# One VectorE rotation for queries and keys, a stabiliser load in four parts, and a written order for the last mLSTM head

## The chip, the core and the metric

The kernel runs on one core of one Trainium2 chip. The metric is the device time of one execution in microseconds; of several executions of a kernel the median is taken. The core has five instruction streams that matter here: TensorE (PE: matmuls, PEld: their weight loads), VectorE (DVE), ScalarE (ACT), GpSimd (POOL) and SyncE (SP), which issues nearly all DMAs. Each engine works through its own stream in order, and waits on semaphores for the others.

## The reference, cut to what matters

One layer of a diffusion backbone: 1024 latent tokens and 256 context tokens of width 1024. After a modulated RMS norm, one projection feeds two groups of heads: a bidirectional chunkwise mLSTM (4 heads of 128) and a windowed attention (8 query heads and 2 key heads of 64). Then w_out, a gated residual, and a ConvGLU of width 2816. The change touches the mLSTM, and the rotary embedding of the attention:

```python
def apply_rope(x, cos, sin):
    b, l, h, _ = x.shape
    xr = x.astype(jnp.float32).reshape(b, l, h, 2, 2, ROPE_AXIS_PAIRS)
    x0, x1 = xr[..., 0, :], xr[..., 1, :]
    cs, sn = cos[:, None], sin[:, None]
    y = jnp.stack([x0 * cs - x1 * sn, x0 * sn + x1 * cs], axis=-2)
    return y.reshape(b, l, h, ATTN_DH).astype(x.dtype)
...
    m_t = jnp.maximum(a_log, jnp.max(d_log, axis=-1))
    dec = jnp.exp(d_log - m_t[..., None])
    inter = jnp.exp(a_log - m_t)
    s = jnp.einsum('bhntd,bhnsd->bhnts', q, k) * dec
...
        y_a = window_attention(apply_rope(qa, cos, sin) * attn_scale, apply_rope(ka, cos, sin), va,
                               ka_c, va_c, attn_sink[l])
```

## The kernel before

Tokens lie in ten chunks of 128: two of context, eight of latents (`NC` = 2, `NL` = 8, `NCH` = 10). A matrix product is made of three (`mm3`: high x high, high x low, low x high parts), so a weight slice arrives raw (`wr`), ScalarE casts the high part (`wh`, L153) and VectorE subtracts the low one (`wl`, L154), each half of a slice apart.

Stages, in us from the start of the span: up to 58 the norms and a first projection; 58 to 100 the second half of the projection of keys, values and gates (`px_mm`, `px_out`), beside the start of head 0's own projections; about 130, 195 and 265 the starts of mLSTM heads 0, 1 and 2, each beside the projections of the next head (`dense`); 334 head 3 (`mlstm(3)`) beside the first query projections (`qgen`); about 369 to 412 the rest of the query projections; from 412 attention and w_out, then the ConvGLU up to 1307.

*`px_out(c)`* evacuates a projected chunk from PSUM: gates on VectorE, `kv` on ScalarE. For latent chunks ScalarE copies the key into `kr`, GpSimd multiplies it with the cosine and sine tables (`rope`) into `ta`, and subtracts and adds the halves into `kv`, which is stored to `kv_d`. Before the projections' second half GpSimd also makes the modulated `ym` (L292) from which VectorE takes the low part `hl` (L297).

*`mlstm(h)`* is a generator of 30 steps: two transpositions ahead (`tr`, L644), nine backward state updates (index `i`; TensorE `pn` L671, VectorE `cst` or `cbk` L679/L681, which the next matmuls need), two forward steps over the context, one `first`, and two for each latent chunk. Its decay tiles `ee` are a broadcast of the stabilisers' rows `m_d`, loaded at its start (L641), masked (`mask`, L654) and exponentiated (`decay`, L658) block by block.

*Between the steps* the loop over heads takes pieces from the generator `dn`: `debt` grows by `rate` at each step (twice at the first), and a piece costs 0.64 if it is six matmuls of a query projection. For heads 0 to 2 `rate` is `RATE` = 1.5; for head 3 it is `RATE3`. In heads 0 to 2 most steps also advance `ada_second`, which loads 256 KB of `w_ada` and multiplies it into `acc` on VectorE (L812, L814).

*`qproj(i, b)`* projects query block `b` of half `i` (24 matmuls of 128x256 in four pieces) and rotates it; `qtrans` splits it into high and low parts `qs`, transposes it (`pt`, L870) and stores it to `q_d` (`QTo`). The 16 blocks come in the order of `qseq`: four of half 0, four of half 1, and so on, so the fifth is the first that needs `w_q[1]`. That slice is loaded at step `LW3` (12) by `late`; its source buffer takes the place of tiles freed at the head's start, and so does the rotated query tile `z`. `row_d` is a 16 KB store of the gate rows (`arw`) just before.

Up to head 2 TensorE, VectorE, ScalarE, GpSimd and SyncE run in the order in which the code is written; in head 3, and up to the last query projection, TensorE alone does, and a scheduler places the others.

Of the kernel before, what the change touches and what calls it, by code (L numbers as in the profile page):

```python
# [73 lines left out]
def build(tc, I, out, dbg=None):  # L74
# [243 lines left out]

    def px_out(c):
# [5 lines left out]
        else:  # L325
            S.copy(kv[:, P:], px[:, 16 + P:XW])
            kr = xp.tile([P, P], F32, name="kr", tag="kr")
            S.copy(kr[:], px[:, 16:16 + P])  # L328
            ta = xp.tile([P, 2, P], F32, name="ta", tag="ta", bufs=1)
            for i in range(2):  # L330
                G.tensor_tensor(out=ta[:, i].rearrange("p (h e) -> p h e", h=KVH),
                                in0=kr[:].rearrange("p (h e) -> p h e", h=KVH),
                                in1=rope[:, i, c - NC].unsqueeze(1).broadcast_to([P, KVH, ADH]), op=ALU.mult)
            tv = ta[:].rearrange("p i (a s j) -> p i a s j", s=2, j=16)
            kvv = kv[:, :P].rearrange("p (a s j) -> p a s j", s=2, j=16)
# [505 lines left out]
    def qproj(i, b):  # L841
# [10 lines left out]
        ta = xp.tile([P, 2 * P], F32, name="ta3", tag="ta", bufs=1)
        q4 = qt.rearrange("p (h e) -> p h e", h=4)
        rp_ = lambda j: rope[:, j, b].unsqueeze(1).broadcast_to([P, 4, ADH])
        G.tensor_tensor(out=ta[:].rearrange("p (h e) -> p h e", h=4), in0=q4, in1=rp_(1), op=ALU.mult)  # L855
        V.tensor_tensor(out=q4, in0=q4, in1=rp_(0), op=ALU.mult)
        tv = ta[:].rearrange("p (a s j) -> p a s j", s=2, j=16)
        qv = qt.rearrange("p (a s j) -> p a s j", s=2, j=16)
        G.tensor_tensor(out=qv[:, :, 0], in0=qv[:, :, 0], in1=tv[:, :, 1], op=ALU.subtract)
        G.tensor_tensor(out=qv[:, :, 1], in0=qv[:, :, 1], in1=tv[:, :, 0], op=ALU.add)  # L860
# [84 lines left out]
    for h in range(H):  # L945
        order_ = {mybir.EngineType.PE}
        if h + 1 < H:
            order_ |= {mybir.EngineType.DVE, mybir.EngineType.Activation, mybir.EngineType.Pool, mybir.EngineType.SP}
        else:
# [16 lines left out]
        with tc.manual_schedule(engines=order_):  # L966
            dn = dense(h + 1, wkq, wvo, *nh) if nh else qgen()
            rate = RATE if nh else RATE3
            for n, _ in enumerate(mlstm(h, *cur)):
# [21 lines left out]
            if nh is None:  # L991
                mstk.close()
                plk.close()
                pl = pT = pa_.enter_context(tc.tile_pool(name="pT", bufs=2, space=PSUM))
                pO = pa_.enter_context(tc.tile_pool(name="pO", bufs=1, space=PSUM))
                pU = pa_.enter_context(tc.tile_pool(name="pU", bufs=1, space=PSUM))
                wm = rstk.enter_context(tc.tile_pool(name="wm", bufs=1, side="right"))
                kT2 = [wm.tile([P, KVH, NCH * P], F32R, name=f"kT2{i}") for i in range(2)]
                vv = wm.tile([P, NCH, KVH, P], F32R, name="vv")
                S.activation(vv[:, 0, 0, 0:1], eps_t[:], AF.Exp)  # L1000
                kgens += [kprep(c) for c in range(NCH)]
                loads += [lambda: load_vv(0), lambda: load_vv(1), lambda: wos.append(load_wo(0, V, wm))]
            for _ in dn:
                pass
# [1042 lines left out]
```

## Time and profile before

| | |
|---|---|
| median of 3 runs | 1310.68 us (1309.24 to 1312.76) |
| the profiled execution | 1308.92 us |
| its span (first to last instruction) | 1306.9 us |
| mean granted TensorE clock | 0.992 |
| busy: PE, PEld, DVE, ACT, POOL | 96%, 82%, 75%, 49%, 19% |

The times of the trace are those of one execution and count from the first instruction of its span. A wait row reads "engine line <- what ended the wait"; PEclk is the granted clock of TensorE as a share of 2.4 GHz.

### The profile page before, as it was taken

The numbers are of one execution on the slowest core, as the hardware profiler recorded it, in microseconds if no ns is written. First come the engines' busy times: TensorE is split into PE (matmuls) and PEld (weight loads), VectorE is DVE, ScalarE is ACT, GpSimd is POOL, SyncE is SP. The second block draws the span as 40 slices with busy tenths as digits, with TensorE's granted clock in tenths as the row PEclk, the third lists the DMA queues.
The fourth block names the chain that finished last, engine by engine and source line by source line (L and its number), as shares of the span: only waits on it lengthen the run. The fifth ranks groups of instructions, "written<-read, shape, count | busy, mean of one in ns | idle before, by whom it ended". The sixth has DMA issues, their size and how long they took to land.

```text
span 1306.9 us, 19479 instructions
## 1 busy us (share of the span) xinstructions
PE 1255.5 (96%) x7071; PEld 1068.6 (82%) x7071; DVE 980.7 (75%) x1752; ACT 635.3 (49%) x1295; POOL 253.1 (19%) x252
## 2 busy tenths in 40 slices
PE   6999999999898999999989999999999999999997
PEld 4789998989898777878768788888888888788886
DVE  5754777777665888897898777777777776867887
ACT  6632546464764666776664333333333333434435
POOL 1240000000134223332411222222212222001000
PEclk9999999999998999999989999999999999999999
DMA  9431535362245322211422333322322326975653
GB/s 362 169 117 35 156 116 149 106 174 73 66 144 179 113 66 97 78 69 64 147 97 97 105 105 105 112 99 105 104 97 105 105 105 235 340 283 165 202 199 130
DMA packets 90226, 175.64 MB, mean 134 GB/s; under 512 B 12746, under 2 KB 29330, under 8 KB 90130
## 3 DMA queue, kind: packets, MB, share of 16 engines
q1 hardware_dynamic: 89842, 173.61, 39.7%
q8 instruction: 56, 0.92, 0.3%
q10 hardware_dynamic: 288, 0.79, 0.2%
q14 instruction: 40, 0.33, 0.1%
HBM read 136.04 MB, written 38.33 MB: 133 GB/s over the span
## 4 chain that ended last, share of the span: by engine, by line
PE 53%; DVE 8%; ACT 3%; DMA 2%; issue 2%; POOL 1%; SPq 0%; ACTq 0%; DVEq 0%; POOLq 0%
PE pd L1892 14%; PE pc L1384 8%; PE pa L1384 8%; PE pe L1384 4%; PE pb L1384 4%; PE pd L1384 4%; PE u L1154 2%; PE po L301 2%; PE po L303 2%; PE po L302 1%; DVE nm L1102 1%; PE pt L1131 1%; DMA ar<-act_s 1%; DVE nm L1103 1%; PE pf L1384 0%
## 5 line engine op out<-in xcount | busy, mean ns | idle before, releaser
L1486 ACT CAST wh<-Rb 128x1024 fp32r<-128x1024 f32 (+1 forms) x66 | 59.5, 904 | 144.6 <-PE pd L1384 81.6
L1892 PE MATMUL pd<-dh,al 128*128 128x512 f32 x296 | 115.5, 390 | 0.8 <-DVE al L1258 0.8
L1892 PE MATMUL pd<-dl,ah 128*128 128x512 f32 x296 | 115.4, 390 | 0.0
L1892 PE MATMUL pd<-dh,ah 128*128 128x512 f32 x296 | 115.3, 389 | 0.0
L1384 PE MATMUL pc<-hB,wh 128*128 128x512 f32 x344 | 106.5, 391 | 1.1 <-DVE av L1463 1.1
L1384 PE MATMUL pa<-hB,wh 128*128 128x512 f32 x336 | 103.7, 390 | 0.0
L1274 DVE TENSOR_TENSOR wl<-Rb,wh 128x1024 fp32r<-128x1024 f32 (+1 forms) x66 | 68.9, 1046 | 39.4 <-ACT wh L1486 38.8
L1594 POOL TENSOR_TENSOR tt<-vt,tt 128x512 f32<-128x512 f32 x22 | 29.5, 1341 | 321.5 <-ACT tt L1588 321.5
L583 PE MATMUL pp<-hl,wh 128*128 128x512 f32 x256 | 79.4, 406 | 1.3 <-ACT kr L328 1.3
L1384 PEld LDWEIGHTS pc<-hB,wh 128*128 128x128 f32 x344 | 64.8, 189 | 15.0 <-DVE av L1463 1.6
L301 PE MATMUL pv<-wh,hl 128*128 128x256 f32 x256 | 76.0, 297 | 0.0
L1384 PEld LDWEIGHTS pa<-hB,wh 128*128 128x128 f32 x336 | 63.0, 188 | 13.4 <-ACT sn L1558 0.4
L303 PE MATMUL pv<-wh,hl 128*128 128x256 f32 x256 | 72.4, 283 | 0.0
L302 PE MATMUL pv<-wl,hl 128*128 128x256 f32 x256 | 72.4, 283 | 0.0
L855 POOL TENSOR_TENSOR ta<-z,rope 128x256 f32<-128x256 f32 x16 | 13.4, 838 | 285.4 <-ACT z L851 285.4
L1384 PE MATMUL pc<-hB,wl 128*128 128x512 f32 x172 | 67.0, 389 | 0.0
L1892 PEld LDWEIGHTS pd<-dh,al 128*128 128x128 f32 x296 | 55.6, 188 | 12.9 <-DVE al L1258 1.5
L1384 PE MATMUL pa<-hB,wl 128*128 128x512 f32 x168 | 65.4, 389 | 0.0
L1892 PEld LDWEIGHTS pd<-dl,ah 128*128 128x128 f32 x296 | 55.6, 188 | 11.9 <-DVE dl L1258 0.3
L1892 PEld LDWEIGHTS pd<-dh,ah 128*128 128x128 f32 x296 | 55.6, 188 | 11.5
L1138 ACT CAST ph<-pt 128x512 fp32r<-128x512 f32 (+1 forms) x88 | 45.3, 526 | 21.8 <-PE pt L1131 21.3
L1102 DVE TENSOR_REDUCE nm<-sps 128x1 f32<-128x640 f32 (+1 forms) x64 | 50.0, 783 | 6.3 <-PE sps L1098 5.7
(1078 smaller groups left out, 3836.4 us busy)
## 6 DMA issues: line engine op xcount, KB each, us to landing
w<-in_w_ada_dram SPq DMA_DIRECT2D x64, 256.0 KB, 2.7
br<-in_w_down_dram SPq DMA_DIRECT2D x25, 512.0 KB, 6.3
Ra<-in_w_up_dram SPq DMA_DIRECT2D x22, 512.0 KB, 3.6
Rb<-in_w_up_dram SPq DMA_DIRECT2D x22, 512.0 KB, 3.6
ar<-act_s SPq DMA_DIRECT2D x44, 256.0 KB, 3.1
act_a<-tt SPq DMA_DIRECT2D x33, 256.0 KB, 2.0
act_s<-tt SPq DMA_DIRECT2D x33, 256.0 KB, 2.0
wr<-in_w_h_dram SPq DMA_DIRECT2D x16, 512.0 KB, 4.4
```

The lines of the kernel that those rows point to most:

```text
L301: T.matmul(ps, st_hi, mv_hi, start=first, stop=False)
L302: T.matmul(ps, st_hi, mv_lo, start=False, stop=False)
L303: T.matmul(ps, st_lo, mv_hi, start=False, stop=last)
L583: T.matmul(pp[:, 512 * n:512 * n + 512], wkq[sw][:, kt, cs], hl[n][part][:, kt, :], start=kt == 0 and sw + part == 0, stop=kt == KT - 1 an ...
L1102: V.tensor_reduce(out=self.nm[:, j:j + 1], in_=self.sv[j], axis=AX.X, op=ALU.max, negate=True)
L1138: S.copy(self.ph[i][:, :w], self.pt[i][:, :w])
L1154: T.matmul(self.u[:], vv[:, c, self.g], part[i][:, kk * 2 * P:(kk + 1) * 2 * P], start=kb + m == 0, stop=kb == last and m == 1)
L1274: sub = lambda e, o, x, y: e.tensor_tensor(out=o, in0=x, in1=y, op=ALU.subtract)
L1384: T.matmul(ps[:], wt[sw][:, j, ks], hB[part][:, blk, kt, :], start=first and kt == 0 and sw + part == 0, stop=last and kt == 3 and sw == 1 ...
L1486: S.copy(wt[0][:], src)
L1594: G.tensor_tensor(out=self.tt[:, h2_], in0=self.vt[:], in1=self.tt[:, h2_], op=ALU.mult)
L1892: T.matmul(ps[:], ac[sa][:, js], w[sw], start=first and n == 0, stop=last and n == 2, skip_group_check=not fresh)
```

## The change

1. A new `rotate` on VectorE does keys and queries in three instructions straight from PSUM: product with the sine table into `ta`, product with the cosine table into the target, and an addition of `ta` with its halves swapped. The sine's sign goes into the table, on the host's side, and the queries' scale moves into `qtrans`.
2. `ee` is loaded in four parts of two blocks, the first at the head's start and the others at steps i = 0, 1 and 2; masks come one step later, and decays later too.
3. The ada pieces of a head start at its step 3 and leave out step 15, where before they left out every eighth step.
4. In head 3 all five engines are in written order; `RATE3` goes from 0.37 to 0.8; `w_q[1]` is loaded in halves at steps 2 and 6 and cut into parts at steps 6 and 10. After the head TensorE alone is in written order, as before.
5. One product of `load_wo` (slice 2) moves from GpSimd to VectorE.

```diff
-RATE3 = 0.37
+RATE3 = 0.8
...
+    def rotate(dst, src, nh, b):
+        ta = xp.tile([P, nh * ADH], F32, name="ta", tag="ta", bufs=1)
+        hv = lambda a: a.rearrange("p (h e) -> p h e", h=nh)
+        sv = lambda a: a.rearrange("p (a s j) -> p a s j", s=2, j=16)
+        for i, o in ((1, ta[:]), (0, dst)):
+            V.tensor_tensor(out=hv(o), in0=hv(src), in1=rope[:, i, b].unsqueeze(1).broadcast_to([P, nh, ADH]), op=ALU.mult)
+        V.tensor_tensor(out=sv(dst), in0=sv(dst), in1=sv(ta[:])[:, :, ::-1], op=ALU.add)
...
-            kr = xp.tile([P, P], F32, name="kr", tag="kr")
-            S.copy(kr[:], px[:, 16:16 + P])
...
-            G.tensor_tensor(out=kvv[:, :, 0], in0=tv[:, 0, :, 0], in1=tv[:, 1, :, 1], op=ALU.subtract)
-            G.tensor_tensor(out=kvv[:, :, 1], in0=tv[:, 1, :, 0], in1=tv[:, 0, :, 1], op=ALU.add)
+            rotate(kv[:, :P], px[:, 16:16 + P], KVH, c - NC)
...
-        nc.sync.dma_start(ee[:], m_d[:].rearrange("(c h) d t -> h c d t", h=H)[h:h + 1, NC:].broadcast_to([P, NL, 2, P]))
+        def ee_load(b):
+            nc.sync.dma_start(ee[:, b:b + 2], m_d[:].rearrange("(c h) d t -> h c d t", h=H)
+                              [h:h + 1, NC + b:NC + b + 2].broadcast_to([P, 2, 2, P]))
+
+        ee_load(0)
...
+            if i < 3:
+                ee_load(2 * i + 2)
             if fins and i:
                 next(fins[0])
-            if i:
-                mask(i - 1)
-            if i and i % 2 == 0:
-                decay(i // 2 - 1)
+            if i > 1:
+                mask(i - 2)
+            if i in (4, 6, 8):
+                decay(i // 2 - 2)
...
-        S.activation(qt, px[:, :256], AF.Copy, scale=float(ADH) ** -0.5)
...
+        rotate(zs[b][:, i], px[:, :256], 4, b)
...
-        S.copy(qs[:, :, 0], qh)
-        V.tensor_tensor(out=qs[:, :, 1], in0=qh, in1=qs[:, :, 0].bitcast(F32), op=ALU.subtract)
+        S.activation(qs[:, :, 0], qh, AF.Copy, scale=float(ADH) ** -0.5)
+        V.scalar_tensor_tensor(out=qs[:, :, 1], in0=qh, scalar=float(ADH) ** -0.5, in1=qs[:, :, 0].bitcast(F32),
+                               op0=ALU.mult, op1=ALU.subtract)
...
-                if nh is None and n == LW3:
-                    late()
+                if nh is None and n == 2:
+                    w1 = load_split(I["w_q"][1], 256, lambda: pq.tile([P, 4, 256], F32, name="wr", tag="rga"), split=False,
+                                    alloc=False, now=(0,))
+                if nh is None and n == 6:
+                    wq.append(w1((0,)))
+                    w1.load(1)
+                if nh is None and n == 10:
+                    w1((1,))
...
-                elif nh and n % 8 != 7:
+                elif nh and n >= 3 and n != 15:
                     next(ada, 0)
```

The first piece of the order is VectorE's stream at the start of head 1, before and then after (`hid` is the tail of head 0, `acc` the ada sums, `cst` the first backward state of the new head):

```order
L737 SCALAR_TENSOR_TENSOR hid<-nm,dn,hid 128x128
L814 SCALAR_TENSOR_TENSOR acc<-w_2229,scc,acc 128x512
L812 TENSOR_SCALAR acc<-w_2268,scc 128x512
L679 COPY cst<-pn 128x129
L154 TENSOR_TENSOR wl<-wr,wh 128x1024
L544 SCALAR_TENSOR_TENSOR kT<-pc__2302,sp,kT 128x255
```

```order
L742 SCALAR_TENSOR_TENSOR hid<-nm,dn,hid 128x128
L682 COPY cst<-pn 128x129
L154 TENSOR_TENSOR wl<-wr,wh 128x1024
L543 SCALAR_TENSOR_TENSOR kT<-pc__2278,sp,kT 128x255
L684 SCALAR_TENSOR_TENSOR cbk<-cst,gd,pn 128x129
L779 RECIPROCAL hss<-hss 128x8
L781 SCALAR_TENSOR_TENSOR ym<-hid,hss,ym 128x128
L821 SCALAR_TENSOR_TENSOR acc<-w_2208,scc,acc 128x512
```

The two sums that stood between the old head's `hid` and the new head's `cst` have moved behind `cbk` and `ym`.

The second piece is SyncE's stream at the start of head 3, before and then after (`wr` are the halves of `w_q[1]`, `ee` the stabilisers' rows, `rga` a broadcast of `row_d`):

```order
L796 DMA w_3575<-in_w_ada_dram 128x512
L641 DMA ee<-m_d 128x8x256
L959 DMA row_d<-arw 32x128
L149 DMA wr<-in_w_q_dram 128x1024 x2
L973 DMA rga<-row_d 128x1024
```

```order
L803 DMA w_3574<-in_w_ada_dram 128x512
L641 DMA ee<-m_d 128x2x256 x2
L953 DMA row_d<-arw 32x128
L149 DMA wr<-in_w_q_dram 128x1024
L641 DMA ee<-m_d 128x2x256 x2
L149 DMA wr<-in_w_q_dram 128x1024
L974 DMA rga<-row_d 128x1024
```

The first half of `w_q[1]` now stands between the second and the third part of `ee`; its issue waits until the store to `row_d` has landed, and the second half's until the first has been cut (both wait the same way before).

The third piece is VectorE's stream in head 3 about the first rotations, before and then after (L856 is the one product of a rotation that VectorE had; L313 and L314 are `rotate`):

```order
L679 COPY cst<-pn 128x129
L693 SCALAR_TENSOR_TENSOR ym<-ym,rw 128x8x128
L681 SCALAR_TENSOR_TENSOR cbk<-cst,gd,pn 128x129
L681 SCALAR_TENSOR_TENSOR cbk<-cbk,gd,pn 128x129
L654 TENSOR_TENSOR ee<-ee,tri 128x256 x2
L681 SCALAR_TENSOR_TENSOR cbk<-cbk,gd,pn 128x129
L654 TENSOR_TENSOR ee<-ee,tri 128x256
```

```order
L682 COPY cst<-pn 128x129
L313 TENSOR_TENSOR ta<-px,rope 128x256
L313 TENSOR_TENSOR z<-px,rope 128x256
L314 TENSOR_TENSOR z<-z,ta 128x256
L684 SCALAR_TENSOR_TENSOR cbk<-cst,gd,pn 128x129
L779 RECIPROCAL hss<-hss 128x8
L781 SCALAR_TENSOR_TENSOR ym<-hid,hss,ym 128x128
L684 SCALAR_TENSOR_TENSOR cbk<-cbk,gd,pn 128x129
L781 SCALAR_TENSOR_TENSOR ym<-hid,hss,ym 128x128
L657 TENSOR_TENSOR ee<-ee,tri 128x256
```

The first mask now stands behind two `cbk`, and the first rotation stands between `cst` and the first `cbk`; the scaling of `ym` (L693) has moved further back.

## Rows read from the trace of the kernel before

**Rows 1.** Engine table of the page: busy time, share of the span, instructions.

```profile
PE 1255.5 (96%) x7071; PEld 1068.6 (82%) x7071; DVE 980.7 (75%) x1752; ACT 635.3 (49%) x1295; POOL 253.1 (19%) x252
```

**Rows 2.** Windows of 20 us: busy time of each engine, PEclk, DMA share, GB/s.

```profile
60.00:80.00 20.00, 17.39 (x130) 16.49 (x129) 8.30 (x25) 8.01 (x23) 13.11 (x26) 1.00 0.36 101
...
340.00:360.00 20.00, 15.82 (x117) 14.84 (x116) 15.75 (x49) 15.05 (x46) 4.06 (x7) 0.91 0.20 64
...
400.00:420.00 20.00, 16.62 (x128) 15.06 (x127) 11.17 (x22) 10.36 (x24) 9.31 (x16) 0.90 0.42 136
420.00:440.00 20.00, 18.27 (x99) 14.77 (x98) 13.80 (x35) 9.20 (x24) 4.08 (x6) 0.93 0.34 119
```

**Rows 3.** Waits of TensorE, 55 to 100 us: total, times, longest.

```profile
PE pa L303 <- DVE hl L297: 1.3, 2, 0.7
PE pp L583 <- ACT kr L328: 1.3, 1, 1.3
```

**Rows 4.** Waits of all engines, 55 to 135 us.

```profile
ACT kv L326 <- DMA kv_d<-kv: 6.2, 2, 5.1
...
DVE hl L297 <- POOL ym L292: 3.5, 2, 2.9
```

**Rows 5.** Waits of all engines, 125 to 335 us.

```profile
DVE acc L812 <- DMA w<-in_w_ada_dram: 9.9, 4, 6.8
...
PE pn L644 <- DVE cst L679: 2.4, 2, 1.2
```

**Rows 6.** Waits of TensorE, 330 to 440 us.

```profile
PE pn L644 <- DVE cbk L681: 2.1, 1, 2.1
PE pn L671 <- ACT kwf L650: 1.6, 3, 1.2
PE pt L870 <- DVE qs L866: 1.5, 3, 0.9
PE pt L870 <- DVE nm L1103: 1.2, 1, 1.2
...
PE pt L870 <- ACT QTo L872: 0.9, 1, 0.9
PE pt L870 <- DVE nm L729: 0.8, 1, 0.8
```

**Rows 7.** Timeline of all engines, 333 to 350 us: start, duration, instruction, [idle before].

```profile
333.68 0.38 SPq L641 DMA_DIRECT2D ee<-m_d  x1
...
334.90 0.33 SPq L959 DMA_DIRECT2D row_d<-arw  x1
...
341.85 0.76 DVE L654 TENSOR_TENSOR ee<-ee,tri 128x256 f32<-128x256 f32 x2 [3.08 <-DMA ee<-m_d]
...
342.13 0.35 SPq L149 DMA_DIRECT2D wr<-in_w_q_dram  x1
```

**Rows 8.** DMA issues, 330 to 420 us: count, KB each, median us to landing.

```profile
ee<-m_d SPq DMA_DIRECT2D x1, 1024.0 KB, 8.1
wr<-in_w_q_dram SPq DMA_DIRECT2D x2, 512.0 KB, 4.1
...
row_d<-arw SPq DMA_DIRECT2D x1, 16.0 KB, 7.1
```

**Rows 9.** VectorE by line, 334 to 372 us: busy us, mean ns, idle before.

```profile
L714 DVE SCALAR_TENSOR_TENSOR ee<-pe,ee 128x256 f32<-128x256 f32 x8 | 3.3, 414 | 0.6 <-PE pe L711 0.6
...
L154 DVE TENSOR_TENSOR wl<-wr,wh 128x1024 fp32r<-128x1024 f32 x2 | 2.7, 1329 | 1.1 <-ACT wh L153 1.1
...
L866 DVE TENSOR_TENSOR qs<-z,qs 128x256 fp32r<-128x256 f32 x4 | 1.6, 410 | 0.0
```

**Rows 10.** VectorE by line, 372 to 412 us.

```profile
L866 DVE TENSOR_TENSOR qs<-z,qs 128x256 fp32r<-128x256 f32 x10 | 6.9, 690 | 6.7 <-ACT qs L865 6.7
```

**Rows 11.** Windows of head 3 and of what follows it.

```profile
334.00:372.00 38.00, 32.64 (x255) 30.85 (x254) 28.50 (x97) 28.93 (x92) 7.15 (x12) 0.96 0.27 78
372.00:412.00 40.00, 38.48 (x335) 37.96 (x335) 23.10 (x48) 21.31 (x52) 21.33 (x33) 1.00 0.60 183
```

More of the change, by code (lines that the diff above doesn't have):

```diff
@@ L326, in px_out @@
             S.copy(kv[:, P:], px[:, 16 + P:XW])
-            kr = xp.tile([P, P], F32, name="kr", tag="kr")
-            S.copy(kr[:], px[:, 16:16 + P])
[L329 to L335, printed above, removed]
-            G.tensor_tensor(out=kvv[:, :, 0], in0=tv[:, 0, :, 0], in1=tv[:, 1, :, 1], op=ALU.subtract)
-            G.tensor_tensor(out=kvv[:, :, 1], in0=tv[:, 1, :, 0], in1=tv[:, 0, :, 1], op=ALU.add)
+            rotate(kv[:, :P], px[:, 16:16 + P], KVH, c - NC)
         nc.sync.dma_start(kv_d[c], kv[:])
@@ L748, in mlstm @@
                 cfs.clear()
-            decay(4 + c)
+            if c == 0:
+                mask(NL - 1)
+            decay(3 + c)
             yield
@@ L759, in mlstm @@
             yield
-            if c < NC + 2:
-                decay(6 + c - NC)
+            if c < NC + 3:
+                decay(5 + c - NC)
             if tail:
@@ L849, in qproj @@
             zs.append(pq.tile([P, 2, 2 * P], F32, name="z", tag="p_", bufs=PB, padded_shape=[P, 2, 320]))
-        qt = zs[b][:, i]
-        S.activation(qt, px[:, :256], AF.Copy, scale=float(ADH) ** -0.5)
[L852 to L860, printed above, removed]
+        rotate(zs[b][:, i], px[:, :256], 4, b)
     def qtrans(i, b):
@@ L945, in build @@
     for h in range(H):
[L946 to L949, printed above, removed]
+        if h + 1 == H:
             wq = [wkq]
-            late = lambda: wq.append(load_split(I["w_q"][1], 256, lambda: pq.tile([P, 4, 256], F32, name="wr", tag="rga")))
             for _ in ada:
@@ L965, in build @@
         debt = 0.0
-        with tc.manual_schedule(engines=order_):
-            dn = dense(h + 1, wkq, wvo, *nh) if nh else qgen()
-            rate = RATE if nh else RATE3
+        rate = RATE if nh else RATE3
+        dn = dense(h + 1, wkq, wvo, *nh) if nh else qgen()
+        with tc.manual_schedule(engines={mybir.EngineType.PE, mybir.EngineType.DVE, mybir.EngineType.Activation,
+                                         mybir.EngineType.Pool, mybir.EngineType.SP}):
             for n, _ in enumerate(mlstm(h, *cur)):
-                if nh is None and n == LW3:
-                    late()
+                if nh is None and n == 2:
[6 more added lines that the diff above has]
+                    w1((1,))
                     rga = pq.tile([P, D], F32, name="rga", tag="rga")
@@ L990, in build @@
                     debt -= w
[L991 to L1004, printed above, removed]
+            if nh:
+                for _ in dn:
+                    pass
+        if nh is None:
+            mstk.close()
+            plk.close()
+            pl = pT = pa_.enter_context(tc.tile_pool(name="pT", bufs=2, space=PSUM))
+            pO = pa_.enter_context(tc.tile_pool(name="pO", bufs=1, space=PSUM))
+            pU = pa_.enter_context(tc.tile_pool(name="pU", bufs=1, space=PSUM))
+            wm = rstk.enter_context(tc.tile_pool(name="wm", bufs=1, side="right"))
+            kT2 = [wm.tile([P, KVH, NCH * P], F32R, name=f"kT2{i}") for i in range(2)]
+            vv = wm.tile([P, NCH, KVH, P], F32R, name="vv")
+            S.activation(vv[:, 0, 0, 0:1], eps_t[:], AF.Exp)
+            kgens += [kprep(c) for c in range(NCH)]
+            loads += [lambda: load_vv(0), lambda: load_vv(1), lambda: wos.append(load_wo(0, V, wm))]
+            with tc.manual_schedule(engines={mybir.EngineType.PE}):
+                for _ in dn:
+                    pass
         cur = nh
@@ L1166, in y2 @@
             V.tensor_tensor(out=yf[64:128], in0=u[64:128, P:2 * P], in1=ut[64:128], op=ALU.add)
-    wos += [load_wo(k, (G, V)[k % 2], lw, "w4") for k in range(1, 4)]
+    wos += [load_wo(k, V, lw, "w4") for k in range(1, 4)]
     w0 = wout_m(0)
@@ L2025, in host_pack @@
     tab = np.stack([np.cos(ang), np.sin(ang)], 0).astype(np.float32)
-    tab = np.repeat(tab[:, :, :, None, :], 2, 3).reshape(2, NL, P, ADH)
+    tab = np.repeat(tab[:, :, :, None, :], 2, 3)
+    tab[1, :, :, 1] *= -1
+    tab = tab.reshape(2, NL, P, ADH)
     r["rope"] = np.ascontiguousarray(tab.transpose(2, 0, 1, 3))
```

## The prediction

> **What bounds the kernel now.** I read the page's engine table first: TensorE is busy for 96% of the span [rows 1], so only time in which it stands, or runs at the lower clock, can be won; the change takes no matmul away. Then I read the windows of 20 us for slices in which TensorE is under 20.00 or PEclk under 1.00, and, in each stretch that the diff touches, the waits of TensorE and those of whoever it waited for. Four places come out.
>
> *Projection of the latent chunks, 55 to 100 us.* TensorE waits 1.3 us for VectorE's `hl` L297 and 1.3 us for ScalarE's `kr` L328 [rows 3]. The first is GpSimd's doing: L297 itself waited 3.5 us for `ym` L292 [rows 4], which stands on GpSimd behind the rotation of a key chunk. The second is a key copy that stood behind `kv`, whose buffer was held by a store that had to wait for GpSimd too (ScalarE: 6.2 us, [rows 4]).
>
> *Starts of mLSTM heads 1 and 2.* TensorE's transposes wait 2.4 us in all for `cst` L679, because the `acc` L812 ahead of it on VectorE waits for its weights, 9.9 us in four waits over three heads [rows 5].
>
> *Head 3, 334 to 372 us.* TensorE waits 2.1 us for `cbk` L681 and 1.6 for `kwf` L650 [rows 6]. Behind both is the 1 MB `ee` load: issued at 333.68, 8.1 us to landing [rows 8]; VectorE's `ee` L654 stands 3.08 us for it, up to 341.85 [rows 7]. The window 340 to 360 then has PEclk 0.91 [rows 2]: at two levels that is 0.09 x 2 x 20 = 3.6 us at 1.2 GHz, up to 1.8 us of work; part of it lies in the waits, so I count 1.5. Loss of the place: 2.1 + 1.6 + 1.5 = 5.2.
>
> *The rest of the query projection and the way into attention, 372 to 430.* 1.5 + 0.8 us for `qs` and `nm`, then 0.9 + 1.2 for `QTo` L872 and L1103 [rows 6]. PEclk 0.90 and 0.93 [rows 2] mean 4.0 + 2.8 us at 1.2 GHz, up to 3.4 us of work.
>
> **The change, part by part.** *Keys rotated on VectorE from PSUM.* GpSimd loses four instructions per chunk, ScalarE the copy. `ym` L292 is then no longer behind anything, and `kv` hangs on two engines instead of three. VectorE gets 8 x 3 instructions of 128 columns; at no more than the 0.41 us that 256 columns cost [rows 9] that is 10 us, spread over 60 to 95, and it is busy for only 8.30 of the 20 us from 60 [rows 2]. Gain between 1.3 (the `hl` waits alone) and 2.6; I take 2.2. Without that idle time the 10 us would push `hl` itself.
>
> *The ada steps start at step 3 of a head.* The first order piece shows it: `cst` no longer has an `acc` ahead of it that waits for a load just issued. The `acc` that now come later have nothing but masks and `cbk` behind them, and a load more time to land. Gain between 0 (the next late thing at a head's start is as late) and 2.4; I take 2.2.
>
> *Four `ee` loads, masks a step later.* Blocks 0 to 3 are 512 KB; at half of 8.1 us they land about 337.8, and `row_d`, 16 KB behind them, about 338.3 instead of 334.90 + 7.1 = 342.0 [rows 7, 8]. The first mask, at step i = 2, is wanted about 340. So the 5.2 us of head 3 can go. In the new SP queue the last two `ee` quarters stand behind the first half of `w_q[1]`, which waits for `row_d`; at the two rates of [rows 8] they land by 338.3 + 4.1 + 4.1 = 346.5 at the latest and are wanted about 347 and 350, so I count nothing for them.
>
> *Head 3 in written order, rate 0.8.* The head's 30 steps and the extra first count make 31 x 0.8 against 31 x 0.37, at 0.64 a chunk of six matmuls: 39 chunks now inside against 18, so 21 x 6 matmuls of 38.48/335 = 0.115 us [rows 11] = 14.5 us move from behind the head into it. TensorE's sum stays. What appears is a wait: the fifth block needs the second half of `w_q[1]` in chunk 19. TensorE gets there after 18 x 0.69 + 11 mLSTM steps of about 0.5 = 17.9 us, at about 352.2. The load's way: first half issued at 338.3, 4.1 us to landing [rows 8], its cast and its `wl` L154 come in the queues at step 7 (about 345), 1.1 + 1.33 us [rows 9], so the buffer is free about 347.3 (second order piece); the second half lands 351.4, cast and L154 end, with half an instruction of their size ahead of them, about 354.4. TensorE stands 2.2 us; nothing hides it, since ScalarE and VectorE stand in the same order. Bounds: 0 (the load is quicker) and 4 (`row_d` late, next part). With 0.3 for small waits in front of it the place gains 5.2 - 2.2 - 0.3 = 2.7.
>
> *Queries rotated on VectorE.* In 334 to 412 VectorE has 28.50 + 23.10 us of work, TensorE 32.64 + 38.48 [rows 11], 69.6 without the half-clock part. Sixteen rotations of three instructions take the place of one such product each: 16 x 2 x 0.41 = 13.1. The nearest rows are a PSUM product with a broadcast operand, 414 ns, and an SBUF one, 410 [rows 9]; no row has the third instruction's reversed pieces of 16, bounded by 0.41 and by what would make VectorE the bound (rivals). `qs` took 690 ns in 372 to 412 [rows 10], where GpSimd works, and 410 before: ten times 0.28 come back. Sum 51.6 + 13.1 - 2.8 = 61.9, 7.7 under TensorE's 69.6, which hides it. The Trainium skill, "GPSIMD Engine Reference", Key points, says that GpSimd shares its SBUF interfaces with VectorE and gets in the way of instructions with two SBUF inputs; the 690 against 410 agrees, and by that rule GpSimd's silence keeps every new instruction at 0.41.
>
> *Behind the head* only TensorE is in written order. There a `pt` stands behind a rotation that waits for a block's end, where before it stood behind GpSimd: from the order I count 1.1 + 0.3 + 1.4 us of such waits against 2.3 now, a loss of 0.4 (between 0 and 2). *Into attention* the chain from the last `px` to the last `pt` loses GpSimd's three steps; of 0.9 + 1.2 I take 1.2, and 0.3 of the clock (bounds 0 and 5.5). The `load_wo` product that moves to VectorE, 128x1024 like L154, lies in the 7.7 us of the last sum; without that cover it costs 1.2.
>
> **Sum:** 2.2 + 2.2 + 2.7 - 0.4 + 1.5 = 8.2 us. The profiled execution took 1308.92 (1306.9 of it span), so 1300.7 by it; it is 1.76 under the median 1310.68, to which the result will be compared, so I forecast **1302.5**, with an own range of 1299.5 to 1304.
>
> **Rivals.** (A) *`row_d` lands at 342 all the same* (small loads may not pass big ones faster). VectorE's write of `z`, the second instruction of the first rotation, waits for that landing, since `z` lies where `row_d`'s source was freed; `cbk` stands behind it, so TensorE's 5.2 us come back in the same place, and the second half's wait disappears in it. 2.2 + 2.2 + 0 - 0.4 + 1.5 = 5.5: 1305.2. For: 7.1 us for 16 KB [rows 8]. Against: that was behind four times the bytes.
>
> (B) *The clock falls at the new wait.* Head 3 shows what follows a stand of 2.1 and 1.2 us: PEclk 0.91 [rows 2, 6]. Another 1.8 us of work at half speed: 1304.3. The Trainium skill, "TensorE: Matmul & The Clock Gate", HAM oscillation, has it that a wait for a load between groups of matmuls can bring the slow clock back; rows 2 agree, and by it alone the time is that 1304.3.
>
> (C) *The waits only change their name*: phase 1 and the head starts find the next late instruction, and 2.7 - 0.4 + 1.5 = 3.8 remain: 1306.9.
>
> (D) *VectorE gets dear.* At the 690 ns of [rows 10] its sum is 61.9 + 48 x 0.28 = 75.3, with 4 us of waits (the 2.2 above and two casts) 79.3 against 78 now: -4.4 + 1.3 = -3.1, so 1307.6. To be **slower** the mean must pass 0.83 us: then 61.9 + 48 x 0.42 = 82.1 plus 4 is 86.1, 8.1 over 78, against the 4.4 won elsewhere. At 0.9 it is 61.9 + 23.5 + 4 - 78 = +11.4, less 4.4: 1317.7. That needs the reversed add at 1.9 us alone; no row is near.
>
> (E) *All clears*: 2.6 + 2.4 + 5.2 - 0.4 + 2.1 + 3.1 = 15: 1295.7.
>
> **How the numbers follow.** Forecast 0.45, A 0.14, B 0.10, C 0.08, D at 0.69 us 0.07, D slower 0.09, E 0.07. What measurement can tell from no change is 0.3%, 3.9 us: faster are the forecast, E, B and two thirds of A, 0.71; within it a third of A, C and the milder D, 0.20; slower 0.09. The range 1297 to 1308 leaves out E and the slower D, 0.16.
>
> **What would show it.** Right: no wait of `pa` L303 and `pp` for `hl` or `kv` in 55 to 100; no wait for `cst` at the head starts; `ee`'s first mask before 340; one wait of about 2 us of a `px` matmul for `wl` about 352; VectorE's rotation at 1.0 to 1.3 us a block; TensorE's stretch from head 3 to the first attention block some 5 us shorter. Wrong: a wait for `row_d` in the first rotation (A); PEclk under 0.95 in 340 to 360 (B); VectorE over 65 us in that stretch (D).

## The result, and the profile after

The changed kernel takes **1300.62 us** in the median of 4 runs (1297.35 to 1302.34); the kernel before, 1311.24 (4 runs, 1309.24 to 1312.76). The ratio is 0.9917, with a 95% interval of 0.9891 to 0.9943: 10.6 us less. The forecast was 1302.5, the range 1297 to 1308. The two profiled executions lie closer together, 1308.92 and 1302.06: the one before was 2.3 us under its median, the one after 1.4 over. The traces therefore account for 6.9 us, 6.6 of it in the span.

How the lead grows, by five points of the two traces:

| us from the start of the span | before | after | lead |
|---|---|---|---|
| first transposition of mLSTM head 0 | 128.2 | 125.6 | 2.6 |
| first `ee` load of head 3 issued | 333.68 | 330.09 | 3.6 |
| last L301 of a query projection | 411.3 | 406.3 | 5.0 |
| first `u` matmul of attention | 425.3 | 419.3 | 6.0 |
| end of the span | 1306.9 | 1300.3 | 6.6 |

The windows of 20 us after, as in [rows 2] (busy time of PE, PEld, DVE, ACT, POOL, then PEclk, DMA share, GB/s):

```profile
60.00:80.00 20.00, 20.00 (x147) 19.26 (x146) 14.89 (x45) 8.81 (x16) 0.55 (x1) 1.00 0.40 126
...
220.00:240.00 20.00, 19.37 (x121) 17.13 (x120) 15.23 (x43) 6.66 (x26) 0.00 (x0) 1.00 0.38 119
...
340.00:360.00 20.00, 17.60 (x148) 16.79 (x147) 18.30 (x54) 13.83 (x36) 0.00 (x0) 1.00 0.27 87
...
380.00:400.00 20.00, 17.39 (x133) 16.58 (x134) 13.59 (x38) 11.28 (x25) 0.00 (x0) 0.91 0.59 174
400.00:420.00 20.00, 17.52 (x122) 14.98 (x120) 17.14 (x36) 11.34 (x24) 1.36 (x2) 0.91 0.72 247
```

From 60 to 80 TensorE is busy for 20.00 us, where it was for 17.39, and GpSimd for 0.55 instead of 13.11. The slice 220 to 240, in the middle of head 1, is new in the list at 19.37 (its like in head 2, 280 to 300, went from 19.81 to 18.91). PEclk is 1.00 in 340 to 360, where it was 0.91, but 0.91 in both slices from 380, where [rows 2] had 0.90 and 0.93 from 400.

TensorE's waits between 125 and 335 after, in place of those of [rows 5]:

```profile
PE pi L730 <- DVE ee L719: 0.6, 1, 0.6
PE pn L704 <- DVE ada L809: 0.6, 1, 0.6
PE pn L704 <- DVE cbk L684: 0.5, 1, 0.5
```

The waits for `cst` are gone, and 1.7 us of others have come. Its waits from 320 to 435, in place of [rows 6]:

```profile
PE pn L647 <- DVE cbk L684: 1.3, 2, 1.1
PE pt L868 <- DVE nm L734: 1.3, 1, 1.3
PE pt L868 <- DVE nm L1108: 1.2, 1, 1.2
PE px L302 <- DVE wl L154: 1.1, 1, 1.1
PE u L842 <- DVE kT L846: 0.9, 1, 0.9
```

Head 3 on all engines after, to set beside [rows 7]:

```profile
335.12 0.42 DVE L313 TENSOR_TENSOR z<-px,rope 128x256 f32<-128x256 f32 x1 [0.18 <-DMA row_d<-arw]
335.17 0.36 SPq L149 DMA_DIRECT2D wr<-in_w_q_dram  x1
...
339.15 0.42 DVE L657 TENSOR_TENSOR ee<-ee,tri 128x256 f32<-128x256 f32 x1
...
343.05 1.23 DVE L154 TENSOR_TENSOR wl<-wr,wh 128x1024 fp32r<-128x1024 f32 x1 [0.32 <-ACT wh L153]
...
344.20 0.34 DVE L684 SCALAR_TENSOR_TENSOR cbk<-cbk,gd,pn 128x129 f32<-128x129 f32 x1
...
344.59 0.33 PE L647 MATMUL pn<-ident,kT 128*128 128x128 f32 x1 [1.14 <-DVE cbk L684]
...
347.93 1.05 ACT L153 CAST wh<-wr 128x1024 fp32r<-128x1024 f32 x1 [1.07 <-DMA wr<-in_w_q_dram]
348.23 1.22 DVE L698 SCALAR_TENSOR_TENSOR ym<-ym,rw 128x1024 f32<-128x1024 f32 x1
...
350.22 1.22 DVE L154 TENSOR_TENSOR wl<-wr,wh 128x1024 fp32r<-128x1024 f32 x1
...
351.49 0.38 PE L302 MATMUL px<-wl,hl 128*128 128x256 f32 x1 [1.12 <-DVE wl L154]
```

`z` waits 0.18 us for `row_d`, which thus lands 3.8 us after its issue at 331.31, and at once the first half of `w_q[1]` is issued. The first mask stands at 339.15, not 341.85. At 343.05 `wl` L154 of that half occupies VectorE for 1.23 us; `cbk` L684 stands behind it, and TensorE waits 1.14 us for `cbk`. The second half is cast by 348.98, but its `wl` starts only at 350.22: in VectorE's written order the scaling of `ym` (L698, 1.22 us) and three short instructions stand ahead of it. Started at 348.98, it would have ended at 350.2, and TensorE wanted it at 351.49 - 1.12 = 350.37. So the wait of 1.1 us is made by the order as much as by the load.

VectorE by line from 328 to 400 (busy us, mean ns, idle before):

```profile
L314 DVE TENSOR_TENSOR z<-z,ta 128x256 f32<-128x256 f32 x13 | 5.5, 423 | 0.3
L863 DVE SCALAR_TENSOR_TENSOR qs<-z,qs 128x256 fp32r<-128x256 f32 x13 | 5.4, 419 | 1.2 <-ACT qs L862 1.2
...
L313 DVE TENSOR_TENSOR z<-px,rope 128x256 f32<-128x256 f32 x13 | 5.4, 413 | 0.2 <-DMA row_d<-arw 0.2
```

A rotation costs 3 x 0.415 us, with 0.02 between the three, so the reversed addition costs what the products do.

### The profile page after: what moved, and what is told of

The parts are those of the page before. It is cut to its first block, busy times and chain, and to the rows that moved or that the text cites. A ratio compares the mean times of both kernels' runs of the same rounds, so it can differ in the third digit from the quotient of the medians.

```text
span 1300.3 us, 19395 instructions
## 1 busy us (share of the span) xinstructions
PE 1253.0 (96%) x7071; PEld 1066.8 (82%) x7071; DVE 993.8 (76%) x1809; ACT 630.7 (49%) x1271; POOL 206.9 (16%) x171
## 4 chain that ended last, share of the span: by engine, by line
PE 52%; DVE 7%; ACT 3%; DMA 3%; issue 1%; POOL 1%; SPq 0%; DVEq 0%; ACTq 0%; POOLq 0%
PE pd L1897 14%; PE pa L1389 9%; PE pc L1389 8%; PE pe L1389 4%; PE pb L1389 4%; PE pd L1389 4%; PE u L1159 2%; PE pt L1136 1%; PE po L301 1%; DMA x<-x_d 1%; DVE hB L1279 1%; PE po L303 1%; PE po L302 1%; DVE nm L1107 1%; DMA wor<-in_w_out_dram 1%
## 5 line engine op out<-in xcount | busy, mean ns | idle before, releaser
L301 PE MATMUL pv<-wh,hl 128*128 128x256 f32 x256 | 75.9, 296 | 0.0
L1389 PEld LDWEIGHTS pa<-hB,wh 128*128 128x128 f32 x336 | 63.0, 188 | 13.5 <-ACT sn L1563 0.4
L1897 PEld LDWEIGHTS pd<-dl,ah 128*128 128x128 f32 x296 | 55.6, 188 | 11.9 <-DVE dl L1263 0.3
L1897 PEld LDWEIGHTS pd<-dh,ah 128*128 128x128 f32 x296 | 55.6, 188 | 11.3
L1389 PE MATMUL pe<-hB,wh 128*128 128x512 f32 x176 | 54.6, 390 | 0.7 <-ACT hB L1349 0.4
```

The source lines that it names most:

```text
L301: T.matmul(ps, st_hi, mv_hi, start=first, stop=False)
L1389: T.matmul(ps[:], wt[sw][:, j, ks], hB[part][:, blk, kt, :], start=first and kt == 0 and sw + part == 0, stop=last and kt == 3 and sw == 1 ...
L1897: T.matmul(ps[:], ac[sa][:, js], w[sw], start=first and n == 0, stop=last and n == 2, skip_group_check=not fresh)
```

## The experiments

There are twelve. Each time is a median, and each ratio is to runs of the kernel before that were taken beside it (medians 1311.2 to 1312.5), with a 95% interval. The changed kernel's own interval is some 7 us wide, so a difference of 2 or 3 us from it is not clear of noise by the times alone; where the traces or a second pair of runs settle it, the text says so.

### Keys back on GpSimd

```diff
-            rotate(kv[:, :P], px[:, 16:16 + P], KVH, c - NC)
+            S.copy(kr[:], px[:, 16:16 + P])
...
+            for s_ in range(2):
+                G.tensor_tensor(out=kvv[:, :, s_], in0=tv[:, 0, :, s_], in1=tv[:, 1, :, 1 - s_], op=ALU.add)
```

> The changed kernel with the key rotation back on GpSimd (ScalarE's copy, two products and two additions per latent chunk); all else as changed. Theory: the 2.6 us by which the first transposition of mLSTM head 0 came earlier (128.2 to 125.6) hang on GpSimd's key work standing ahead of ym and holding kv; then the waits of pa for hl (about 1.3) and of pp for kr (about 1.3) come back and head 0 starts at 128.0 to 128.5, the end 2.0 to 2.6 us later than the changed kernel's 1300.3 of span. Rival: the gain came from the ada load that no longer stands between the stores of kv; then head 0 still starts before 126.5 and the two waits stay under 0.6 us together.

Measured: 1303.83 us (ratio 0.9938, 0.9925 to 0.9950), 3.2 more by medians, with overlapping intervals. TensorE's waits from 55 to 100:

```profile
PE pa L303 <- DVE hl L297: 1.3, 2, 0.7
PE pp L592 <- ACT kr L337: 1.3, 1, 1.3
```

These are the two rows of [rows 3] again, to the tenth. The theory holds: 2.6 us are two waits with GpSimd behind them. Head 0 starts at 129.1, later than the 128.0 to 128.5 expected. The other traces bear the step out: the first transposition of head 0 comes at 124.8 to 125.6 in all eleven kernels in which VectorE rotates the keys, and at 128.2, 128.6 and 129.1 in the three in which GpSimd does.

### The old rule for the ada steps

```diff
-                elif nh and n >= 3 and n != 15:
+                elif nh and n % 8 != 7:
```

> The changed kernel with the old rule for the ada steps (all but every eighth step of a head). Theory: the sum behind a fresh load stands ahead of cst again at the starts of heads 1 and 2, TensorE waits there 2.0 to 2.4 us for cst, and the waits that the changed kernel has in mid-head instead (0.6 for ee L719, 0.6 for ada L809, 0.5 for cbk) vanish: head 3 starts 0.5 to 1.5 us later than in the changed kernel, 200 us after head 0 has begun. Rival: with ee in four parts the weights ahead of cst land in time whatever the rule, since 1 MB no longer stands before them in the queue; then no wait for cst over 0.5 us, and head 3 starts up to 1.7 us earlier.

Measured: 1298.14 us (0.9897, 0.9884 to 0.9909), some 2.5 *less* than with the new rule by medians, though the intervals overlap. The window 125 to 330 of this kernel, and of the changed one:

```profile
125.00:330.00 205.00, 205.00 (x1481) 191.67 (x1480) 148.95 (x361) 110.23 (x316) 0.00 (x0) 1.00 0.42 125
```

```profile
125.00:330.00 205.00, 203.28 (x1459) 189.30 (x1458) 147.78 (x357) 107.76 (x309) 0.00 (x0) 1.00 0.41 124
```

With the old rule TensorE does not stand at all in these 205 us. VectorE at the start of head 1 shows why, first in the kernel before, then here:

```profile
204.95 0.49 DVE L812 TENSOR_SCALAR acc<-w,scc 128x512 f32<-128x512 f32 x1 [6.83 <-DMA w<-in_w_ada_dram]
205.35 0.28 DVE L679 COPY cst<-pn 128x129 f32<-128x129 f32 x1
```

```profile
197.13 0.48 DVE L819 TENSOR_SCALAR acc<-w,scc 128x512 f32<-128x512 f32 x1 [0.55 <-DMA w<-in_w_ada_dram]
198.40 0.29 DVE L682 COPY cst<-pn 128x129 f32<-128x129 f32 x1 [0.78 <-PE pn L674]
```

The sum `acc` L819 does stand ahead of `cst`, as before the change, but it waits 0.55 us for its weights, not 6.83. The rival holds: with `ee` in four parts the head starts are cured whatever the rule; the new rule cured nothing that was left, and brought the 1.7 us in mid-head.

That the rule costs something is clear from all traces together. From the first transposition of head 0 to the first `ee` load of head 3 it takes 201.9 us in each of the four kernels with four loads and the old rule, 204.1 to 205.4 in the eight with the new rule, and 205.5 and 204.5 in the two with one load and the old rule.

### One load of the stabilisers' rows

```diff
-            nc.sync.dma_start(ee[:, b:b + 2], m_d[:].rearrange("(c h) d t -> h c d t", h=H)
-                              [h:h + 1, NC + b:NC + b + 2].broadcast_to([P, 2, 2, P]))
+            nc.sync.dma_start(ee[:], m_d[:].rearrange("(c h) d t -> h c d t", h=H)[h:h + 1, NC:].broadcast_to([P, NL, 2, P]))
...
-            if i < 3:
-                ee_load(2 * i + 2)
```

> The changed kernel with the stabilisers' rows in one load of 1 MB at the head's start, masks and decays still a step later. Theory: row_d lands about 7 us after its issue instead of 3.8, the first rotation's second product waits for it some 3 us with cbk behind it, the first half of w_q[1] is issued at 338 instead of 335, and TensorE waits 2 to 4 us more in head 3 (for cbk, kwf or wl), with PEclk under 1.00 in 340 to 360; end 2 to 5 us later. At the starts of heads 1 and 2 nothing changes, since the sums of ada stand behind cst. Rival: the later masks alone give the load its time and row_d is not slowed by it; then the wait for row_d stays under 0.5 us and the end moves by under 0.7.

Measured: 1301.58 us (0.9931, 0.9918 to 0.9943), a span of 1302.9. The wait of VectorE in 325 to 362, and the loads' times to landing in 325 to 360:

```profile
DVE z L313 <- DMA row_d<-arw: 3.5, 1, 3.5
```

```profile
ee<-m_d SPq DMA_DIRECT2D x1, 1024.0 KB, 8.2
...
row_d<-arw SPq DMA_DIRECT2D x1, 16.0 KB, 7.1
```

The mechanism is as expected: 16 KB behind 1 MB land after 7.1 us, behind 512 KB after 3.8; `z` stands 3.5 us and `cbk` with it (TensorE waits 2.1 for it, 1.3 in the changed kernel). PEclk is 0.91 in 340 to 360. The size is at the low end or under it: 1.0 us by medians, which the two intervals cannot tell from nothing, and 2.6 by the spans of single executions. At the starts of heads 1 and 2 there is no wait for `cst` here either, with one load and the new rule: either of the two cures is enough for it.

### Rate and written order: four corners

Rate 0.37 with all engines in written order:

```diff
-RATE3 = 0.8
+RATE3 = 0.37
```

> The changed kernel with the rate of query projection pieces in head 3 at 0.37 again (18 pieces in the head instead of 39). Theory: TensorE has the same matmuls, and the gain of this stretch came from the waits for ee and the order, not from the rate: the wait for wl (1.1) is gone, as the fifth block starts later, cbk waits are 0 to 2, and the end moves by -1 to +2 us. Rival: the pieces are what covers mLSTM's chain between the engines; with half of them TensorE waits 3 us or more for cbk, kwf, cst or nm in head 3, PEclk falls, and the end is 3 to 7 us later.

Rate 0.8 with TensorE alone in written order:

```diff
-        with tc.manual_schedule(engines={mybir.EngineType.PE, mybir.EngineType.DVE, mybir.EngineType.Activation,
-                                         mybir.EngineType.Pool, mybir.EngineType.SP}):
+        with tc.manual_schedule(engines={mybir.EngineType.PE, mybir.EngineType.DVE, mybir.EngineType.Activation,
+                                         mybir.EngineType.Pool, mybir.EngineType.SP} if nh else {mybir.EngineType.PE}):
```

> The changed kernel, but in head 3 only TensorE is in written order and the scheduler places VectorE, ScalarE, GpSimd and SyncE, as before; rate 0.8 and all else as changed. With rate 0.37 in full written order the time was that of the kernel before, so either the rate alone carries the gain of head 3, or rate and order together. Theory: the rate alone; TensorE waits under 5 us in 325 to 432 and the time is within 2 us of the changed kernel's 1300.6. Rival: the scheduler puts the rotations and wl where mLSTM's chain stands behind them; waits of 8 us or more there, PEclk under 1.00 in head 3, and 1304 or more.

Rate 0.37 with TensorE alone in written order (both edits):

> The changed kernel with TensorE alone in written order in head 3, and the rate at 0.37. It is the fourth corner beside the changed kernel (all in order, 0.8: 1300.6), rate 0.37 in full order (1311.6) and TensorE in order at 0.8 (1297.8). Theory: the two are not additive; the scheduler fits the sparse order of rate 0.37 as it did in the kernel before, only the waits for ee, hl and cst are gone: 1302 to 1305, TensorE waits 3 to 6 us in 325 to 432. Rival: the rate is worth 11 us in any order: 1307 to 1310, with PEclk under 1.00 in 340 to 380.

| head 3 | rate 0.37 | rate 0.8 |
|---|---|---|
| five engines in written order | 1311.59, ratio 1.0002 (0.9993 to 1.0012) | 1300.62, ratio 0.9917 (0.9891 to 0.9943) |
| TensorE alone in written order | 1298.06, ratio 0.9889 (0.9874 to 0.9904) | 1297.84, ratio 0.9890 (0.9872 to 0.9909) |

All three expectations missed somewhere. With the scheduler the rate is worth nothing. In written order it is worth 11 us, and even then the order costs about 3; here the intervals at 0.8 overlap, but with the old ada rule the same pair of orders is apart beyond them (1298.14 against 1293.57, last experiment). TensorE's waits in 325 to 380 of the first, and one of its windows:

```profile
PE pn L647 <- DVE cbk L684: 4.1, 4, 2.2
PE pt L868 <- DVE nm L734: 3.4, 1, 3.4
```

```profile
340.00:360.00 20.00, 15.61 (x113) 14.86 (x114) 16.92 (x50) 11.62 (x37) 0.00 (x0) 0.91 0.16 53
```

With 18 pieces in the head, mLSTM's chain runs through five queues in a fixed order with too little beside it; TensorE stands some 11 us (the rows shown and smaller ones) and runs part of the time at 1.2 GHz (PEclk 0.91 also in 360 to 380). Which of the other four queues costs most was not run apart. The scheduler at rate 0.8 leaves little inside head 3; the longest wait there is:

```profile
PE pn L674 <- ACT kwf L653: 0.9, 1, 0.9
```

### Queries back on GpSimd

```diff
-        rotate(zs[b][:, i], px[:, :256], 4, b)
+        S.copy(qt, px[:, :256])
...
+        G.tensor_tensor(out=ta[:].rearrange("p (h e) -> p h e", h=4), in0=q4, in1=rp_(1), op=ALU.mult)
+        V.tensor_tensor(out=q4, in0=q4, in1=rp_(0), op=ALU.mult)
...
+        for s_ in range(2):
+            G.tensor_tensor(out=qv[:, :, s_], in0=qv[:, :, s_], in1=tv[:, :, 1 - s_], op=ALU.add)
```

> The changed kernel with the query rotation as before (ScalarE copy, GpSimd product, VectorE product, two GpSimd additions; the scale stays in qtrans), keys still on VectorE. Theory: in written order ScalarE's qs stands for GpSimd's last addition (16.2 us of such waits in the kernel before) and holds mLSTM's activations behind it, so TensorE waits 2 to 6 us more in head 3 and after, and qs is slowed beside GpSimd again (0.69 instead of 0.42 us): 1302.5 to 1306. Rival: the two blocks by which qtrans lags cover the longer chain, VectorE's 13 us less make up for it: within 1.5 us of 1300.6.

Measured: 1308.51 us (0.9971, 0.9960 to 0.9983), 7.9 more than the changed kernel. TensorE's waits, and ScalarE's, in 325 to 440:

```profile
PE pt L878 <- ACT QTo L880: 6.0, 3, 3.6
...
PE pt L878 <- ACT kT L845: 1.8, 1, 1.8
```

```profile
ACT qs L872 <- POOL z L867: 11.0, 6, 2.6
```

The theory's mechanism (ScalarE's `qs` behind GpSimd, 11.0 us) holds, at more than the expected price; PEclk is 0.91, 0.83 and 0.91 in the three slices from 380, against 0.91, 0.91 and 1.00 in the changed kernel, so part of the 7.9 us is the lower clock behind these waits. The part on `qs` fell: it took 0.42 us (see the last section).

### The rate and an early w_q on the kernel before

```diff
-RATE3 = 0.37
+RATE3 = 0.8
...
-LW3 = 12
+LW3 = 2
```

> The kernel before with two numbers changed: the rate in head 3 at 0.8 and w_q[1] loaded at step 2 instead of 12; queries and keys still rotated by GpSimd among others, one ee load, scheduler as before. Theory: the rate needs the rotation on VectorE (with GpSimd's rotation in full order the changed kernel lost 8 us); GpSimd's three instructions a block, 2 us and more, come at every 3.9 us of TensorE's, and qs waits for them: -2 to +3 us against the kernel before, 1309 to 1314. Rival: the rate alone carries head 3's gain whoever rotates: 1304 to 1307.

Measured: 1318.23 us (1.0045, 1.0032 to 1.0057), 5.8 us slower than the kernel before by medians. TensorE's waits in 325 to 440:

```profile
PE pt L870 <- ACT QTo L872: 3.2, 2, 2.3
PE pt L870 <- DVE qs L866: 2.9, 1, 2.9
PE pn L644 <- DVE cbk L681: 2.7, 1, 2.7
```

With the rate up, the load early and GpSimd's rotation, the kernel loses. The direction of the theory holds, at a higher price than its range, but its mechanism is not shown: ScalarE's `qs` waits 15.2 us for GpSimd in 325 to 440, no more than the 16.2 of the kernel before. Besides, ScalarE's copy `z` waits 3.0 us for the one load of `ee`, by the profile, and PEclk is 0.74 in 420 to 440 (0.93 before). The run changes the rate and the load of `w_q[1]` together and keeps the one `ee` load, so it does not tell which of these costs the 5.8 us, nor that the rate needs the rotation on VectorE.

### Every query rotation twice

```diff
         rotate(zs[b][:, i], px[:, :256], 4, b)
+        rotate(zs[b][:, i], px[:, :256], 4, b)
```

> The changed kernel with every query rotation done twice (the same three instructions once more with the same result): 48 instructions of 0.415 us, 19.9 us more for VectorE. In 330 to 407 it is busy 58.9 us now, TensorE 71.2 of 77. Theory of the prediction (VectorE stands 7.7 us and more under TensorE, and becomes the bound at a mean of 0.57 us an instruction): 58.9 + 19.9 = 78.8 passes TensorE, so the stretch grows by 4 to 10 us, TensorE waits for nm, cbk and ee, and the time is 1305 to 1311. Rival: VectorE waits so much itself that the added work fills holes; time within 2 us of 1300.6.

Measured: 1316.09 us (1.0030, 1.0018 to 1.0042), 15.5 more than the changed kernel for 19.9 us of added VectorE work. The changed kernel's window from 330 to 407, then this one's from 329 to 420, and TensorE's waits from 325 to 440:

```profile
330.00:407.00 77.00, 71.19 (x592) 69.16 (x591) 58.86 (x175) 47.15 (x130) 0.00 (x0) 0.98 0.40 127
```

```profile
329.00:420.00 91.00, 78.03 (x607) 74.25 (x605) 75.41 (x219) 48.14 (x132) 0.00 (x0) 0.94 0.37 114
```

```profile
PE pt L869 <- DVE qs L864: 5.0, 2, 2.8
PE pt L869 <- DVE nm L734: 4.2, 3, 3.4
PE pn L647 <- DVE cbk L684: 2.1, 2, 1.4
```

TensorE now waits for VectorE most, and only about 4 us of the added work is hidden. Not all of the rest is VectorE's own: the last L301 of a query projection comes 11.3 us later (417.6), and PEclk fell too, to 0.94 over the window and 0.83 in 420 to 440. The cover was thinner than the difference of the two busy sums (71.19 - 58.86 = 12.3), and VectorE is not full even here, busy for 75.4 of 91 us: it too waits for others, 6.1 us of it for ScalarE with `nm`.

### The second half of w_q[1] earlier

Old ada rule, and:

```diff
-                if nh is None and n == 6:
+                if nh is None and n == 4:
...
-                if nh is None and n == 10:
+                if nh is None and n == 9:
```

> The changed kernel with the old rule for the ada steps (which gave 1298.1) and w_q[1] cut at steps 4 and 9 instead of 6 and 10, so that its second half is issued some 3 us earlier. Theory: the wait of px for wl (1.1 us) is the second half's landing plus its cast, so it goes; the wait for cbk behind the first half's L154 (1.1 us) may stay: 1296.5 to 1297.5. Rival: at step 4 the first half has not landed yet, ScalarE and VectorE stand for it in their queues, and TensorE waits 1 to 3 us more for cbk: 1298 to 1300.

Measured: 1298.47 us (0.9899, 0.9879 to 0.9918), against 1298.14 with the old ada rule alone. TensorE's waits:

```profile
PE pn L647 <- DVE cbk L684: 2.2, 3, 1.1
...
PE px L302 <- DVE wl L154: 0.2, 1, 0.2
```

The wait for `wl` went from 1.1 to 0.2, and that for `cbk` from 1.3 (with the old rule alone too) to 2.2. The wait was moved, and the time stayed. The theory's cause was only half of it: here too `wl` stands behind `ym` L698 (345.36, then `wl` at 346.50), though the cast is done by 344.95.

### The best version, and one step further

The old ada rule with TensorE alone in written order in head 3, at rate 0.8:

> The changed kernel with the old rule for the ada steps and, in head 3, TensorE alone in written order (rate 0.8). Apart they gave 1298.1 and 1297.8 against 1300.6. Theory: the two act in different stages (125 to 330 and 330 to 410), so they add: 1295 to 1296. Rival: the slow-clock stretch at the start of attention, which all of these kernels have, takes part of it back: 1296.5 to 1298.

Measured: **1293.57 us** (0.9855, 0.9841 to 0.9868), the fastest of all: it beats both kernels. The two gains add, and the sum came out a little larger than expected (1295 to 1296). Against this kernel each of the two parts is clear of noise by its interval: the order against 1298.14 (0.9884 to 0.9909), the ada rule, by a hair, against 1297.84 (0.9872 to 0.9909).

With the rate at 1.0 and the cuts at steps 4 and 9 besides:

> comb2 with the rate at 1.0 (48 of 64 pieces in head 3 instead of 39) and w_q[1] cut at steps 4 and 9. Theory: TensorE waits little inside head 3 already, so more pieces there change nothing inside and leave fewer behind the head, where kprep's and qtrans' waits then have less to stand beside: within 1.5 us of comb2. Rival: as from 0.37 to 0.8, each piece covers a wait: 2 us or more under comb2.

Measured: 1298.41 (0.9896, 0.9882 to 0.9909), 4.8 more. The expectation fell on its far side. TensorE's waits behind head 3:

```profile
PE u L842 <- DVE kT L846: 2.9, 2, 1.6
PE sps L1096 <- DMA QT<-q_d: 1.6, 1, 1.6
```

At rate 0.8 (1293.57) these rows are 0.3 for `kT` and none for `q_d`. With fewer blocks left behind the head, `kprep`'s chain and attention's first load of `q_d` have too little beside them: 48 pieces are too many, while 18 and 39 came out alike under the scheduler. The cuts were moved in the same run; they changed nothing under the written order, but were not run apart here.

## Why the prediction was right, and where not

The time, the sign and the size came out; the sum did so partly by errors that cancel.

*Keys on VectorE* (2.2): right in mechanism, 2.6 in the trace; undoing it brings both waits back.

*The ada steps* (2.2): this step failed. Heads 0 to 2 gained 1.0 net, and did not need the rule for it. The prediction said that the `acc` that come later "have nothing but masks and `cbk` behind them", but `ee` L719 and the `ada` total stand there too, and `cbk` itself was waited for: 1.7 us in all. That is the prediction's own rival C, come true at this one place. And the prediction gave the cure of `cst` to the rule alone, where `ee` in four parts does it too, and without the new waits: the weights are no longer queued behind 1 MB. In [rows 5] the wait is for the DMA, and the prediction moved the waiter without asking what the load waited for.

*Four loads* (the 5.2 of head 3): the mechanism is shown by the single load. `row_d` landed 3.8 us after issue (forecast: 338.3 - 334.9 = 3.4), the first mask stood ahead of 340, PEclk was 1.00 in 340 to 360. Rivals A and B did not come. The size of 5.2 is not shown: with the one load back, and the masks still a step later, the time grew by 1.0 to 2.6 us only.

*Rate and written order* (a new wait of 2.2, and 0.3): TensorE waited 1.1 for `wl` at 351.5 and 1.3 for `cbk`, 2.4 in all. The term's size is right by chance, for its parts were not. The load came as forecast, 17.8 us after the head's first `ee` load (forecast 351.4 - 333.7 = 17.7); what stood ahead of `wl` in VectorE's order cost 1.2, where half an instruction, 0.6, was counted, and TensorE came later than counted, partly for its wait behind the first half's `wl`. (The 1.1 taken from [rows 9] for the cast is VectorE's wait for it; the cast itself took 1.04.) What the prediction lacked is a price for the order itself: it wrote that "TensorE's sum stays" and counted one late load. The corners show that the order costs about 3 us at rate 0.8 and some 13.5 at 0.37, and that with the scheduler the rate makes no difference. The prediction did say why ("ScalarE and VectorE stand in the same order"), but priced it only where a DMA was late.

*Queries on VectorE* (hidden, at 0.41 an instruction): right, 0.413 to 0.423; VectorE's sum was 58.9 instead of 61.9. Rival D's point, 0.83 an instruction, was reached by doing each rotation twice: 1.0030, which is the 0.3% that the point stood for. That the ratio agrees is partly luck: D counts 8.1 - 4.4 + 8.2 = 11.9 us over the forecast, the run cost 15.5 over the changed kernel. And the prediction counted no gain for the queries other than 1.5 at the way into attention; taken back to GpSimd at this rate and order they cost 7.9.

*Behind the head* (-0.4) *and into attention* (1.5): the waits are much as counted, 1.3 for `nm`, 0.3 for `QTo`, 0.2 for `qs` and 0.9 for `kT`, 2.7 in all where 1.1 + 0.3 + 1.4 was forecast; the last is the key preparation's wait, not a rotation's. The slow clock stayed and came 20 us earlier. Head 3 and what follows it gained 1.4 (2.3 forecast), the way into attention 1.0. The sign "some 5 us shorter", for the stretch from head 3 to the first attention block, did not fit the prediction's own sum for it (2.7 - 0.4 + 1.5 = 3.8); it is 2.4 shorter.

So 2.6 + 1.0 + 1.4 + 1.0 = 6.0 where 8.2 was forecast for the place up to the first `u`, and 0.6 behind it. That the medians differ by 10.6 rather than 6.9 lies in the scatter between executions, as far as is known, which the traces cannot divide among the steps. Three things stay open: what the queries' rotation is worth at rate 0.37 with the scheduler was not run; the later masks and the moved `load_wo` product were never undone by themselves; and what makes the slow-clock stretch at the start of attention, which every version has, was not taken apart.

## What to carry to other kernels

When a change carries several edits against the same wait, run the corners: here one of two cures was enough and the other cost 2.5 us, and beside a written order the new rate looked like a gain where it only repaired what the order broke. Here a chain that crosses engines paid for a fixed order although no engine was full; let the engines off the critical one be scheduled, unless a run shows the gain. Before an instruction is moved from behind a late load, ask what makes the load late.
